# A row-sum kernel on one core: GpSimd scales the results, and the input is read in two parts at other pitches

## The chip, the core and the metric

The kernel runs on one core of a Trainium2 chip. VectorE, ScalarE and GpSimd are the engines that compute here. The DMA engines move data between HBM, where the input and the output lie, and SBUF, where the kernel's tiles of 128 partitions lie; SyncE issues these transfers. A load "lands" when all of its data has arrived. The metric is the device time of one execution in microseconds (us). The profile's span, from the first to the last instruction, is some 1.6 us shorter than that time (159.8 against 161.4 for the kernel before).

## The reference

```python
batch, seq, dim = 32, 512, 1024
x = np.random.randn(batch, seq, dim).astype(np.float32)
divisor = float(dim)
return (np.sum(x, axis=-1) / divisor).astype(np.float32)
```

There are 16,384 rows of 1024 float32, 64 MB (67.11 million bytes) in all. On 128 partitions that is 128 rows per partition. One row on every partition is 512 KB, and "one row" below means that.

## The kernel before

112 rows per partition come first, 448 KB apart from partition to partition. The last 16 rows per partition lie in a part of their own, 64 KB apart. All loads go through one queue (the page has one, q1, with 2592 packets, the stores among them). VectorE sums most rows, ScalarE some of the last, and a first store writes 112 columns while the last loads still arrive. The end is cut finely so that little work is left when the last byte lands.

```python
L = 16
M = J - L                                   # 112
x_main = bass.AP(tensor=x.tensor, offset=0, ap=[[M * D, P], [D, M], [1, D]])
x_last = bass.AP(tensor=x.tensor, offset=P * M * D, ap=[[L * D, P], [D, L], [1, D]])
main = [(2, 0)] + [(14, 0)] * 6 + [(14, 4), (12, 5)]      # (rows, of these on ScalarE)
last = [(8, 4), (4, 2), (2, 1)]
bulk = ctx.enter_context(tc.tile_pool(name="bulk", bufs=3))   # three large buffers
one = ctx.enter_context(tc.tile_pool(name="one", bufs=1))
res = one.tile([P, M], F32, name="res")
fin = one.tile([P, L], F32, name="fin")
q = one.tile([P, L], F32, name="q")
r = one.tile([P, L], F32, name="r")
nc.gpsimd.memset(r, 0.0)
# ... loads and sums; the 4-row and 2-row loads and the row below have tiles of pool "one"
c = 768
row = one.tile([P, D], F32, name="row")
load(row, x_last[:, j, :])
act_sum(r[:, j : j + 1], row[:, c:], by=scale)
nc.vector.reduce_sum(out=q[:, j : j + 1], in_=row[:, :c], axis=AX)
# ... the last row comes in three pieces: pa (448 columns), pb (256), pc (320)
nc.gpsimd.tensor_scalar_mul(out=res, in0=res, scalar1=scale)
tc.keep_in_program_order(nc.sync.dma_start(out=o_main, in_=res))
act_sum(pc[:, D - b : D - b + 1], pa)
nc.vector.reduce_sum(out=pc[:, D - b + 1 :], in_=pb, axis=AX)
nc.vector.scalar_tensor_tensor(out=fin[:, : L - 1], in0=q[:, : L - 1], scalar=scale,
                               in1=r[:, : L - 1], op0=MULT, op1=ADD)
nc.vector.tensor_scalar(out=scaled, in0=pc, scalar1=scale, scalar2=0.0, op0=MULT, op1=ADD,
                        accum_out=fin[:, L - 1 :])
tc.keep_in_program_order(nc.sync.dma_start(out=o_last, in_=fin))
```

Of the kernel before, what the change touches and what calls it, by code (L numbers as in the profile page):

```python
# [9 lines left out]
F32 = mybir.dt.float32  # L10
ADD = mybir.AluOpType.add
MULT = mybir.AluOpType.mult
# [55 lines left out]
def close_while_storing(nc, landed):  # L68


    body, end = nc.main_func.blocks[1], nc.main_func.blocks[-1]
    store = [i for i in body.instructions if i.engine == SP and type(i).__name__ == "InstDMACopy"][-1]
    (lane,) = store.sync_info.on_update
    drain = end.instructions[0]
    assert drain.engine == SP and type(drain).__name__ == "InstDrain"
    needs = {w.id: w for w in drain.sync_info.on_wait}
    assert needs[lane.id].wait_value > lane.update_value
    needs[lane.id] = dataclasses.replace(
        needs[lane.id], wait_value=needs[lane.id].wait_value - lane.update_value
    )  # L80

    (done,) = [w for w in store.sync_info.on_wait if w.ant_name.startswith("DVE_")]
    assert needs[done.id].wait_value == done.wait_value
    del needs[done.id]
    own = dict(sync_type="semaphore", id=landed.num, ant_name=landed.name)
    add = mybir.SyncUpdate(update_mode="sem-add-imm", update_value=16, **own)
    sub = mybir.SyncUpdate(update_mode="sem-sub-imm", update_value=16, **own)
    last = nc.sync.wait_ge(landed, 16).ins
    assert nc.main_func.blocks[-1].instructions[-1].name == last.name
    body.instructions = [i for i in body.instructions if i.name != store.name]  # L90
    end.instructions = [
        with_sync(drain, on_wait=tuple(needs.values())),
        with_sync(store, on_wait=(done,), on_update=(add,)),
        *end.instructions[1:-1],
        with_sync(last, on_update=(sub,)),
    ]


@with_exitstack
def kernel(  # L100
    ctx: ExitStack,
    tc: tile.TileContext,
    x: bass.AP,
    divisor: float,
    out: bass.AP,
):
    nc = tc.nc
    landed = nc.alloc_semaphore("landed")
    nc.at_finalize(start_loads_at_once)
    nc.at_finalize(latest_wait_first)  # L110
    nc.at_finalize(lambda nc: close_while_storing(nc, landed))
    xf = x.flatten_outer_dims()
    N, D = xf.shape
    P = nc.NUM_PARTITIONS
    scale = 1.0 / float(divisor)
    J = N // P
    assert J * P == N


    L = 16  # L120
    M = J - L
    x_main = bass.AP(tensor=x.tensor, offset=0, ap=[[M * D, P], [D, M], [1, D]])
    x_last = bass.AP(tensor=x.tensor, offset=P * M * D, ap=[[L * D, P], [D, L], [1, D]])
    o_main = bass.AP(tensor=out.tensor, offset=0, ap=[[M, P], [1, M]])
    o_last = bass.AP(tensor=out.tensor, offset=P * M, ap=[[L, P], [1, L]])


    main = [(2, 0)] + [(14, 0)] * 6 + [(14, 4), (12, 5)]
    last = [(8, 4), (4, 2), (2, 1)]
    assert sum(n for n, _ in main) == M and sum(n for n, _ in last) == L - 2  # L130
    bulk = ctx.enter_context(tc.tile_pool(name="bulk", bufs=3))
    one = ctx.enter_context(tc.tile_pool(name="one", bufs=1))
    psum = ctx.enter_context(tc.tile_pool(name="junk", bufs=4, space=bass.MemoryType.PSUM))

    res = one.tile([P, M], F32, name="res")
    fin = one.tile([P, L], F32, name="fin")
    q = one.tile([P, L], F32, name="q")
    r = one.tile([P, L], F32, name="r")
    nc.gpsimd.memset(r, 0.0)  # L139

    def load(dst, src):
        tc.keep_in_program_order(nc.sync.dma_start(out=dst, in_=src))  # L142

    def act_sum(dst, src, by=1.0):
        n = src.shape[-1]
        junk = psum.tile([P, D], F32, name="junk")
        nc.scalar.activation(junk[:, :n], src, COPY, scale=by, accum_out=dst)  # L147

    def sums(dst, t, rows, on_act):
        d = rows - on_act  # L150
        for i in range(d, rows):
            act_sum(dst[:, i : i + 1], t[:, i, :])
        nc.vector.reduce_sum(out=dst[:, :d], in_=t[:, :d, :], axis=AX)  # L153

    j = 0
    for rows, on_act in main:
        t = bulk.tile([P, 14, D], F32, name="t")
        load(t[:, :rows, :], x_main[:, j : j + rows, :])
        sums(res[:, j : j + rows], t, rows, on_act)
        j += rows  # L160
    j = 0
    for rows, on_act in last:
        if rows == 8:
            t = bulk.tile([P, 14, D], F32, name="t")[:, :8, :]
        else:
            t = one.tile([P, rows, D], F32, name=f"t{rows}")
        load(t, x_last[:, j : j + rows, :])
        sums(q[:, j : j + rows], t, rows, on_act)
        j += rows


    c = 768
    row = one.tile([P, D], F32, name="row")
    load(row, x_last[:, j, :])
    act_sum(r[:, j : j + 1], row[:, c:], by=scale)
    nc.vector.reduce_sum(out=q[:, j : j + 1], in_=row[:, :c], axis=AX)  # L176



    a, b = 448, 704  # L180
    pa = one.tile([P, a], F32, name="pa")
    pb = one.tile([P, b - a], F32, name="pb")
    pc = one.tile([P, D - b + 2], F32, name="pc")
    load(pa, x_last[:, L - 1, :a])
    load(pb, x_last[:, L - 1, a:b])
    load(pc[:, : D - b], x_last[:, L - 1, b:])


    nc.gpsimd.tensor_scalar_mul(out=res, in0=res, scalar1=scale)  # L189
    tc.keep_in_program_order(nc.sync.dma_start(out=o_main, in_=res))  # L190

    act_sum(pc[:, D - b : D - b + 1], pa)
    nc.vector.reduce_sum(out=pc[:, D - b + 1 :], in_=pb, axis=AX)  # L193
    nc.vector.scalar_tensor_tensor(  # L194
        out=fin[:, : L - 1], in0=q[:, : L - 1], scalar=scale, in1=r[:, : L - 1], op0=MULT, op1=ADD
    )
    scaled = one.tile([P, D - b + 2], F32, name="scaled")
    nc.vector.tensor_scalar(  # L198
        out=scaled, in0=pc, scalar1=scale, scalar2=0.0, op0=MULT, op1=ADD, accum_out=fin[:, L - 1 :]
    )  # L200
    tc.keep_in_program_order(nc.sync.dma_start(out=o_last, in_=fin))
# [35 lines left out]
```

## Time and profile before

| | before |
|---|---|
| time, median of the first 3 runs | 161.4 us |
| span of the profiled run | 159.8 us |
| read from HBM | 67.11 MB |
| VectorE / ScalarE / GpSimd busy | 76% / 12% / 0% |
| 14-row loads land every | 16.94 us |
| VectorE needs for one | 15.09 us |
| last full row lands at | 156.16 us |
| last VectorE result at | 158.28 us |

The busy shares name no bound. The landings do: where its engine is free, a load's first reader starts about 0.02 us after it lands, so the starts of the readers in the timeline are the clock of the transfer. The prediction shows these lines and reads them.

### The profile page before, as it was taken

Reading aid. Unit: us, or ns where it says so; the run is one execution under the profiler, and the core shown is the slowest. Engines: PE = TensorE matmul, PEld = TensorE weight load, DVE = VectorE, ACT = ScalarE, POOL = GpSimd, SP = SyncE. Lnnn points to the kernel's source line nnn. Section 1 sums busy time; section 2 is a strip of 40 time slices with the busy share of each in tenths; the row PEclk is TensorE's granted clock in tenths of the full one; section 3 lists DMA queues with packets and bytes.
Section 4 is the critical chain, followed back from the end, with each engine's and each line's share of the span. In section 5 each row is a group of like instructions: output and inputs, shape, how many; then the busy total and the mean of one; then the engine's idle time right before and its main releaser. Section 6 shows DMA issues by size and latency. Waiting matters only on the chain.

```text
span 159.8 us, 139 instructions
## 1 busy us (share of the span) xinstructions
DVE 121.1 (76%) x17; ACT 19.6 (12%) x37; POOL 0.8 (0%) x6
## 2 busy tenths in 40 slices
DVE  0500059995999599978999599959995996494985
ACT  3000000000000000000000000000001900480973
POOL 0000000000000000000000000000000000001000
DMA  7999999978999999978999999978999999899993
GB/s 250 472 459 459 459 459 459 459 330 359 459 459 459 459 459 459 459 316 373 459 459 459 459 459 459 416 345 388 459 459 427 394 480 505 353 435 390 408 400 132
DMA packets 2592, 67.18 MB, mean 420 GB/s; under 512 B 544, under 2 KB 928, under 8 KB 1056
## 3 DMA queue, kind: packets, MB, share of 16 engines
q1 hardware_dynamic: 2592, 67.18, 98.0%
HBM read 67.11 MB, written 0.07 MB: 420 GB/s over the span
## 4 chain that ended last, share of the span: by engine, by line
DMA 76%; DVE 22%; SPq 1%; issue 0%; DVEq 0%
DMA t<-in_x_dram 56%; DMA row<-in_x_dram 21%; DVE res L153 20%; SPq L142 1%; DVE q L176 1%; DVE scaled L198 0%; DVE pc L193 0%; DVE fin L194 0%; DVEq L198 0%; DVEq L232 0%
## 5 line engine op out<-in xcount | busy, mean ns | idle before, releaser
L153 DVE TENSOR_REDUCE res<-t 128x14 f32<-128x14336 f32 (+3 forms) x9 | 111.2, 12360 | 34.3 <-DMA t<-in_x_dram 34.3
L147 ACT ACTIVATE junk<-t 128x1024 f32<-128x1024 f32 x16 | 16.2, 1013 | 135.9 <-DMA t<-in_x_dram 135.9
L153 DVE TENSOR_REDUCE q<-t 128x4 f32<-128x4096 f32 (+2 forms) x3 | 7.9, 2642 | 2.7 <-DMA t<-in_x_dram 2.5
L147 ACT ACTIVATION_READ_ACCUMULATOR junk<-t 128x1 f32 x16 | 3.0, 187 | 0.0
L147 ACT ACT_TABLE_LOAD x1 | 1.3, 1283 | 1.7 <-PEq L218 1.7
L189 POOL TENSOR_SCALAR res<-res 128x112 f32<-128x112 f32 x1 | 0.5, 494 | 143.8 <-DVE res L153 143.8
L176 DVE TENSOR_REDUCE q<-row 128x1 f32<-128x768 f32 x1 | 1.0, 953 | 0.0
L198 DVE TENSOR_SCALAR_CACHE_REDUCE scaled<-pc 128x322 f32<-128x322 f32 x1 | 0.5, 490 | 0.1
L147 ACT ACTIVATE junk<-pa 128x448 f32<-128x448 f32 x1 | 0.5, 548 | 0.0
L193 DVE TENSOR_REDUCE pc<-pb 128x1 f32<-128x256 f32 x1 | 0.4, 414 | 0.0
L147 ACT ACTIVATE junk<-row 128x256 f32<-128x256 f32 x1 | 0.4, 388 | 0.1
L194 DVE SCALAR_TENSOR_TENSOR fin<-q,r 128x15 f32<-128x15 f32 x1 | 0.2, 176 | 0.0
L147 ACT ACTIVATION_READ_ACCUMULATOR junk<-pa 128x1 f32 x1 | 0.2, 186 | 0.0
L147 ACT ACTIVATION_READ_ACCUMULATOR junk<-row 128x1 f32 x1 | 0.2, 185 | 0.0
L139 POOL MEMSET r<- 128x16 f32 x1 | 0.1, 112 | 1.3 <-POOLq L218 1.3
L218 POOL MEMSET const-bfloat16-1.0<- 128x1 bf16 x1 | 0.1, 103 | 0.0
L218 POOL MEMSET const-uint8-127<- 128x1 uint8 x1 | 0.1, 102 | 0.0
L218 POOL MEMSET const-float32-0.0<- 128x1 f32 x1 | 0.1, 99 | 0.2 <-issue 0.2
L218 POOL MEMSET const-float32-1.0<- 128x1 f32 x1 | 0.1, 99 | 0.0
L198 DVE DVE_READ_ACCUMULATOR scaled<-pc 128x1 f32 x1 | 0.1, 83 | 0.0
## 6 DMA issues: line engine op xcount, KB each, us to landing
t<-in_x_dram SPq DMA_DIRECT2D x7, 7168.0 KB, 35.7
t<-in_x_dram SPq DMA_DIRECT2D x1, 6144.0 KB, 33.3
t<-in_x_dram SPq DMA_DIRECT2D x1, 4096.0 KB, 26.1
t<-in_x_dram SPq DMA_DIRECT2D x2, 1024.0 KB, 18.6
t<-in_x_dram SPq DMA_DIRECT2D x1, 2048.0 KB, 30.5
row<-in_x_dram SPq DMA_DIRECT2D x1, 512.0 KB, 33.2
pa<-in_x_dram SPq DMA_DIRECT2D x1, 224.0 KB, 33.3
pc<-in_x_dram SPq DMA_DIRECT2D x1, 160.0 KB, 33.1
```

The costliest lines, as they stand in the source:

```text
L139: nc.gpsimd.memset(r, 0.0)
L142: tc.keep_in_program_order(nc.sync.dma_start(out=dst, in_=src))
L147: nc.scalar.activation(junk[:, :n], src, COPY, scale=by, accum_out=dst)
L153: nc.vector.reduce_sum(out=dst[:, :d], in_=t[:, :d, :], axis=AX)
L176: nc.vector.reduce_sum(out=q[:, j : j + 1], in_=row[:, :c], axis=AX)
L189: nc.gpsimd.tensor_scalar_mul(out=res, in0=res, scalar1=scale)
L193: nc.vector.reduce_sum(out=pc[:, D - b + 1 :], in_=pb, axis=AX)
L194: nc.vector.scalar_tensor_tensor(out=fin[:, : L - 1], in0=q[:, : L - 1], scalar=scale, in1=r[:, : L - 1], op0=MULT, op1=ADD)
L198: nc.vector.tensor_scalar(out=scaled, in0=pc, scalar1=scale, scalar2=0.0, op0=MULT, op1=ADD, accum_out=fin[:, L - 1 :])
L218: nc = _bacc.Bacc("TRN2", target_bir_lowering=False, num_devices=1)
```

## The change

Its intent is to take two short things off the end of VectorE's work. GpSimd scales the last columns, and ScalarE takes 64 more columns of the last full row. It also rearranges which rows each partition reads. The first 16 rows per partition become a part of their own, 64 KB apart. The other 112 lie 448 KB apart, and their last 16 are the tail.

```diff
-    L = 16
-    M = J - L
-    x_main = bass.AP(tensor=x.tensor, offset=0, ap=[[M * D, P], [D, M], [1, D]])
-    x_last = bass.AP(tensor=x.tensor, offset=P * M * D, ap=[[L * D, P], [D, L], [1, D]])
+    F, L = 16, 16
+    M = J - F - L
+    W = M + L
+    x_first = bass.AP(tensor=x.tensor, offset=0, ap=[[F * D, P], [D, F], [1, D]])
+    x_main = bass.AP(tensor=x.tensor, offset=P * F * D, ap=[[W * D, P], [D, M], [1, D]])
+    x_last = bass.AP(tensor=x.tensor, offset=P * F * D + M * D, ap=[[W * D, P], [D, L], [1, D]])
 ... (outputs likewise; the loads are split into first and main, sizes and order kept)
+    res0 = one.tile([P, F], F32, name="res0")
     res = one.tile([P, M], F32, name="res")
-    r = one.tile([P, L], F32, name="r")
-    nc.gpsimd.memset(r, 0.0)
+    r = one.tile([P, 1], F32, name="r")
 ...
-    c = 768
+    c = 704
-    act_sum(r[:, j : j + 1], row[:, c:], by=scale)
+    act_sum(r, row[:, c:], by=scale)
 ...
+    tc.keep_in_program_order(nc.sync.dma_start(out=o_first, in_=res0))
     tc.keep_in_program_order(nc.sync.dma_start(out=o_main, in_=res))
 ...
-    nc.vector.scalar_tensor_tensor(
-        out=fin[:, : L - 1], in0=q[:, : L - 1], scalar=scale, in1=r[:, : L - 1], op0=MULT, op1=ADD
+    nc.gpsimd.tensor_scalar_mul(out=fin[:, :j], in0=q[:, :j], scalar1=scale)
+    nc.gpsimd.tensor_scalar(
+        out=fin[:, j : j + 1], in0=q[:, j : j + 1], scalar1=scale, scalar2=r, op0=MULT, op1=ADD
     )
```

More of the change, by code (lines that the diff above doesn't have):

```diff
@@ L117 @@
     assert J * P == N
-    L = 16
-    M = J - L
-    x_main = bass.AP(tensor=x.tensor, offset=0, ap=[[M * D, P], [D, M], [1, D]])
-    x_last = bass.AP(tensor=x.tensor, offset=P * M * D, ap=[[L * D, P], [D, L], [1, D]])
-    o_main = bass.AP(tensor=out.tensor, offset=0, ap=[[M, P], [1, M]])
-    o_last = bass.AP(tensor=out.tensor, offset=P * M, ap=[[L, P], [1, L]])
-    main = [(2, 0)] + [(14, 0)] * 6 + [(14, 4), (12, 5)]
+    F, L = 16, 16
[4 more added lines that the diff above has]
+    x_last = bass.AP(tensor=x.tensor, offset=P * F * D + M * D, ap=[[W * D, P], [D, L], [1, D]])
+    o_first = bass.AP(tensor=out.tensor, offset=0, ap=[[F, P], [1, F]])
+    o_main = bass.AP(tensor=out.tensor, offset=P * F, ap=[[W, P], [1, M]])
+    o_last = bass.AP(tensor=out.tensor, offset=P * F + M, ap=[[W, P], [1, L]])
+    first = [(2, 0), (14, 0)]
+    main = [(14, 0)] * 5 + [(14, 4), (12, 5)]
     last = [(8, 4), (4, 2), (2, 1)]
+    assert sum(n for n, _ in first) == F
     assert sum(n for n, _ in main) == M and sum(n for n, _ in last) == L - 2
@@ L153, in sums @@
         nc.vector.reduce_sum(out=dst[:, :d], in_=t[:, :d, :], axis=AX)
-    j = 0
-    for rows, on_act in main:
-        t = bulk.tile([P, 14, D], F32, name="t")
-        load(t[:, :rows, :], x_main[:, j : j + rows, :])
-        sums(res[:, j : j + rows], t, rows, on_act)
-        j += rows
+    for loads, src, dst in ((first, x_first, res0), (main, x_main, res)):
+        j = 0
+        for rows, on_act in loads:
+            t = bulk.tile([P, 14, D], F32, name="t")
+            load(t[:, :rows, :], src[:, j : j + rows, :])
+            sums(dst[:, j : j + rows], t, rows, on_act)
+            j += rows
+        nc.gpsimd.tensor_scalar_mul(out=dst, in0=dst, scalar1=scale)
     j = 0
@@ L186 @@
     load(pc[:, : D - b], x_last[:, L - 1, b:])
-    nc.gpsimd.tensor_scalar_mul(out=res, in0=res, scalar1=scale)
+    tc.keep_in_program_order(nc.sync.dma_start(out=o_first, in_=res0))
     tc.keep_in_program_order(nc.sync.dma_start(out=o_main, in_=res))
```

## The prediction

> **What bounds the kernel now.** I read the page first (busy shares and bytes), then the timeline for the moments at which loads land, then the chain of work that ended last for the tail, then the SyncE queue's own waits for the end of the program. The page:
>
> ```profile
> span 159.8 us, 139 instructions
> ...
> DVE 121.1 (76%) x17; ACT 19.6 (12%) x37; POOL 0.8 (0%) x6
> ...
> HBM read 67.11 MB, written 0.07 MB: 420 GB/s over the span
> ```
>
> No engine is full: VectorE has a quarter of the span free, GpSimd is idle. What is large is the bytes. Whether the transfers stream without a hole is read from the timeline, because each reduction starts as its load lands:
>
> ```profile
> 4.83 2.29 DVE L153 TENSOR_REDUCE res<-t 128x2 f32<-128x2048 f32 x1 [4.83 <-DMA t<-in_x_dram]
> 21.76 15.09 DVE L153 TENSOR_REDUCE res<-t 128x14 f32<-128x14336 f32 x1 [14.65 <-DMA t<-in_x_dram]
> 38.71 15.09 DVE L153 TENSOR_REDUCE res<-t 128x14 f32<-128x14336 f32 x1 [1.87 <-DMA t<-in_x_dram]
> ...
> 106.47 15.09 DVE L153 TENSOR_REDUCE res<-t 128x14 f32<-128x14336 f32 x1 [1.85 <-DMA t<-in_x_dram]
> ...
> 137.94 7.62 DVE L153 TENSOR_REDUCE res<-t 128x7 f32<-128x7168 f32 x1 [3.72 <-DMA t<-in_x_dram]
> ...
> 147.66 4.42 DVE L153 TENSOR_REDUCE q<-t 128x4 f32<-128x4096 f32 x1 [2.09 <-DMA t<-in_x_dram]
> ```
>
> From 21.76 to 106.47 five loads of 14 rows land, 16.94 us each. That is 1.210 us a row (512 KB over all partitions), 7,340,032 bytes / 16.94 us = 433 GB/s. VectorE needs 15.09 for what takes 16.94 to arrive, and waits some 1.85 us for each load. The tail keeps the same pace: the 8-row load lands 147.66 - 137.94 = 9.72 us after the one before it, 1.215 a row; and that one already comes from the part whose partitions lie 64 KB apart. So the kernel is one unbroken transfer: 128 rows x 1.210 = 154.9 us, before it 4.83 - 2 x 1.210 = 2.41 us until the stream is at its pace, and after it a tail. 2.41 + 154.9 = 157.3; the rest of 159.8, 2.5 us, is what the kernel does after its last byte.
>
> The head, in the view by windows (columns: window, length, busy time of DVE, ACT and POOL, clock, DMA share, GB/s):
>
> ```profile
> 0.00:2.00 2.00, 0.00 (x0) 0.26 (x1) 0.30 (x5) 1.00 0.49 90
> 2.00:4.00 2.00, 0.00 (x0) 1.02 (x1) 0.00 (x0) 1.00 0.97 410
> ```
>
> In the first two microseconds the DMA engines are half busy and move little. The trace's records of single packets say why: the first 8 KB packet of each engine takes 0.43 to 1.29 us, from the third on each takes 0.31. The slowest engine loses about 1 us there[...]. The tail, in the chain (start, us, what):
>
> ```profile
> 122.91 33.25 DMA row<-in_x_dram
> ...
> 156.18 0.96 DVE q L176
> 157.14 0.03 issue
> 157.17 0.18 DVE fin L194
> 157.34 0.34 DVE pc L193
> 157.68 0.04 DVEq L198
> 157.72 0.07 issue
> 157.79 0.49 DVE scaled L198
> ```
>
> VectorE carries four instructions in a row after the landing of the last full row at 156.16. The final store is issued at 158.31 and lands about 1.4 us later. Before it, the SyncE queue also waits for the earlier transfers:
>
> ```profile
> SPq L190 <- DMA t<-in_x_dram: 13.1, 1, 13.1
> ...
> SPq L232 <- DMA out_dram<-res: 0.6, 1, 0.6
> ...
> SPq L201 <- DVE scaled L198: 0.5, 1, 0.5
> ```
>
> The last line is the slack: all other transfers were done 0.5 us before the last VectorE result.
>
> [...]
>
> **The change, part by part.**
> *Bulk.* The loads keep their sizes and order (2, seven of 14, 12, 8, 4, 2, 1, and the last row in three pieces), the tiles and the three buffers too. Only addresses change. The first 16 rows get the 64 KB pitch that the last 16 had, the last 16 the 448 KB pitch that the main part had. Both pitches run at full rate in the trace. Effect: 0 us.
>
> *Head.* The first packets now touch 128 places in 8 MB instead of 56 MB. If the slow first packets depend on how far apart the places are, up to a few tenths change; if they are a cold start of the engines, nothing. I take -0.05 us.
>
> *Scaling of the first part.* One small GpSimd instruction near 37 us instead of its share of the one at 145.65. Off the path: 0 us. The store of the first part is one more transfer. The 13.1 us wait above shows a store that waits for a load eight transfers before it (the one that landed at 137.94). So the new first store will wait until about 137.9 and the main store until the 8-row load at 147.7, instead of 146.17. [...]the main store landed at about 157.7. Eight more packets of 64 bytes per engine at 11 ns each (packet records) put it at 157.8. The final store is not ready before 158.1, so this is hidden: 0 us.
>
> *Tail on VectorE.* Removed: the 176 ns multiply-add, of which about 0.09 us stands on the path, since the next reduction starts 0.09 after it (157.26 against 157.17). Shortened: the row reduction from 768 to 704 columns. With 1220 ns at 1024 and 953 at 768 a column costs 1.04 ns, so 64 columns give 0.07 us: 953 becomes 886. ScalarE takes 320 instead of 256 columns; with 388 ns at 256 and 548 at 448 that is 441 ns. It ends near 156.62, and its next instruction moves from 156.72 to about 156.77, its result from 157.39 to about 157.44. New times: row reduction 156.18 to 157.07; reduction of pb (landed near 157.0) 157.10 to 157.51; scaled, 0.12 after it as before, from 157.63 (pc landed near 157.5) to 158.12. Before: 158.28. Gain: 0.16 us.
>
> *Tail on GpSimd.* The 14 scaled columns can start when the one-row reduction is done, near 156.2. The last column's multiply-add starts after the row reduction, near 157.15. From 494 ns for 112 columns, and 112 ns for a memset of 16 columns, I estimate 0.25 to 0.45 us for each. The last ends at 157.4 to 157.6, half a microsecond before 158.12: hidden.
>
> *Final store.* 64 bytes per partition as before, but 448 bytes apart instead of side by side. I expect its landing within 0.1 us of 1.4.
>
> Sum: -0.05 - 0.16 = -0.21 us. Span 159.55; time 161.4 - 0.2 = 161.2 us.
>
> **The rivals.**
> *GpSimd sets the end.* If its last instruction took over 0.9 us, or if the framework made VectorE's write of the last column wait for GpSimd's writes to the same tile, the end would move to about 158.5 or later: +0.2 to +0.6, 161.6 to 162.0. Against it: at 123.41 ScalarE and VectorE write columns of the same tile together, so columns are kept apart, and 494 ns for eight times the columns leaves room.
> *The 64 KB pitch hurts the large pieces.* The last part read 32 KB pieces and smaller at that pitch; now 56 KB pieces are read.[...] Against it: 9.72 us for eight rows at that pitch.
> *A better head or tail.* The 4 KB packets of the last full row took 172 ns on average where the quickest took 159: 13 ns x 8 = 0.1 us per engine, at the 64 KB pitch. A wider pitch may take that away, and a tighter one may spare half of the lost 1 us at the head: 160.6 to 161.0.
>
> **Range and chances.** [...]the result can leave 161.4 only by the head (at most 1 us) and the tail (some tenths). Runs of before lie within 0.17 us. I predict 161.2, range 160.6 to 161.7. Faster by 2% means below 158.2; the data alone end at 157.3 in the span, and the time is 1.6 us more than the span (161.4 against 159.8), which makes 158.9 even without a tail: 0.01. Slower by 2% means over 164.6, which only the pitch rival gives: 0.01. Same: 0.98.
>
> **What would show it.** In the changed profile: 14-row loads 16.94 us apart, also the first; first load near 4.8; row reduction near 886 ns; the reduction of pb right behind it; scaled ending near 158.1; the final store released by VectorE, not GpSimd or a store; span near 159.6. Wrong if a landing interval exceeds 1.22 us a row (pitch), if the first landing moves by over 0.3 us (head), or if GpSimd stands in the chain at the end.

The forecast's sum came to -0.21 us, -0.05 from the head (a guess) and -0.16 from the tail on VectorE. That no layout could make the bulk faster was the assumption. The trace shows 1.210 us a row (433 GB/s) at 448 KB and 1.215 at 64 KB, and these are the "full rate" under *Bulk*. No measured figure stands behind the 64 KB rival's time over 164.6.

## The result, and the profile after

The changed kernel took 161.37 us (median of 6 runs, 161.22 to 161.61) and the kernel before 161.31 (6 runs, 161.25 to 161.51). The ratio is 1.0002, with a 95% interval of 0.999 to 1.0015: the same. A ratio here is the mean time of one kernel's fast runs over that of the other's of the same rounds, so it is not quite the ratio of the medians. Executions over 1.5% slower than the fastest of the same kernel are left out of the means.

The changed kernel's page:

```profile
span 159.9 us, 143 instructions
...
DVE 121.0 (76%) x16; ACT 19.7 (12%) x37; POOL 1.4 (1%) x8
...
HBM read 67.11 MB, written 0.07 MB: 420 GB/s over the span
```

VectorE has one instruction less and GpSimd two more. The bytes are the same. The timeline of the changed kernel (start, us, engine, line, operation, output from input, count, idle time before and what ended it), at the head and at the end:

```profile
4.92 2.29 DVE L158 TENSOR_REDUCE res<-t 128x2 f32<-128x2048 f32 x1 [4.92 <-DMA t<-in_x_dram]
21.86 15.09 DVE L158 TENSOR_REDUCE res<-t 128x14 f32<-128x14336 f32 x1 [14.66 <-DMA t<-in_x_dram]
38.81 15.09 DVE L158 TENSOR_REDUCE res<-t 128x14 f32<-128x14336 f32 x1 [1.86 <-DMA t<-in_x_dram]
...
147.76 4.42 DVE L158 TENSOR_REDUCE q<-t 128x4 f32<-128x4096 f32 x1 [2.09 <-DMA t<-in_x_dram]
...
152.65 2.29 DVE L158 TENSOR_REDUCE q<-t 128x2 f32<-128x2048 f32 x1 [0.47 <-DMA t<-in_x_dram]
...
155.15 1.22 DVE L158 TENSOR_REDUCE q<-t 128x1 f32<-128x1024 f32 x1 [0.21 <-DMA t<-in_x_dram]
...
156.46 0.89 DVE L183 TENSOR_REDUCE q<-row 128x1 f32<-128x704 f32 x1
```

The bulk is as before: 14-row loads 16.94 to 16.95 us apart, also in the part at 64 KB. The tail is not. From the 8-row load on, the next three landings come 4.89, 2.50 and 1.31 us apart. Before they were 4.84, 2.42 and 1.26. There the readers of these loads started at 147.66 and 156.18 (both in the prediction's lines), and between them on ScalarE:

```profile
152.49 1.03 ACT L147 ACTIVATE junk<-t 128x1024 f32<-128x1024 f32 x1 [0.57 <-DMA t<-in_x_dram]
...
154.92 1.03 ACT L147 ACTIVATE junk<-t 128x1024 f32<-128x1024 f32 x1 [0.24 <-DMA t<-in_x_dram]
```

The chain of the changed kernel shows what the later landings do to the end (start, us, what):

```profile
123.98 33.43 DMA pb<-in_x_dram
...
157.43 0.43 DVE pc L200
...
157.97 0.49 DVE scaled L206
```

The reduction of pb now waits for a landing (157.41) where it should have followed VectorE's own work. The row reduction is shorter and ended at 156.46 + 0.89 = 157.35, but pb was not there yet.

The book of the two profiled runs, up to the end of `scaled` (158.28 before, 158.46 after, so +0.18):

- First landing: 4.83 to 4.92, +0.09.
- From the first landing to the start of the row reduction: 151.35 to 151.54, +0.19.
- From there to the end of `scaled`: 2.10 to 2.00, -0.10.

So the end did become shorter, and the transfers took the gain back before it. The question for the experiments is what made them later.

### The profile page after: what moved, and what is told of

It is laid out like the page before. It is cut to its first block, busy times and chain, and to the rows that moved or that the text cites. A ratio compares the mean times of both kernels' runs of the same rounds, so it can differ in the third digit from the quotient of the medians.

```text
span 159.9 us, 143 instructions
## 1 busy us (share of the span) xinstructions
DVE 121.0 (76%) x16; ACT 19.7 (12%) x37; POOL 1.4 (1%) x8
## 4 chain that ended last, share of the span: by engine, by line
DMA 77%; DVE 21%; SPq 1%; issue 0%; DVEq 0%
DMA t<-in_x_dram 56%; DMA pb<-in_x_dram 21%; DVE res L158 20%; SPq L147 1%; DVE scaled L206 0%; DVE pc L200 0%; DVEq L206 0%; DVEq L240 0%
## 5 line engine op out<-in xcount | busy, mean ns | idle before, releaser
L167 POOL TENSOR_SCALAR res<-res 128x16 f32<-128x16 f32 (+1 forms) x2 | 0.7, 354 | 145.1 <-DVE res L158 145.1
L183 DVE TENSOR_REDUCE q<-row 128x1 f32<-128x704 f32 x1 | 0.9, 885 | 0.1
```

The lines of the kernel that those rows point to most:

```text
L167: nc.gpsimd.tensor_scalar_mul(out=dst, in0=dst, scalar1=scale)
```

## The experiments

Three theories were on the table first. A: the new addresses make the small pieces of the tail slower. B: the landings set the end anyway, and the work taken off VectorE was never worth anything. C: the later landings were chance. "Landings" below are the three intervals after the 8-row load (of the 4-row, the 2-row and the one-row load), read from the starts of their readers.

### The end alone, and the addresses alone

`tail_only` is the kernel before with the change's end and nothing of its layout:

```diff
-    r = one.tile([P, L], F32, name="r")
-    nc.gpsimd.memset(r, 0.0)
+    r = one.tile([P, 1], F32, name="r")
-    c = 768
+    c = 704
-    nc.vector.scalar_tensor_tensor(out=fin[:, : L - 1], ...)
+    nc.gpsimd.tensor_scalar_mul(out=fin[:, :j], in0=q[:, :j], scalar1=scale)
+    nc.gpsimd.tensor_scalar(out=fin[:, j : j + 1], ..., scalar2=r, op0=MULT, op1=ADD)
```

> Addresses, parts and stores of before; only the end is that of the change (GpSimd scales the last 15 columns, row split at 704). Theory A, the gain on VectorE is real and the new addresses took it back: row reduction about 885 ns, reduction of pb right behind it near 157.1, scaled ends near 158.1, time 0.16 us under before (ratio about 0.999). Rival B, the landing of the last pieces sets the end and the VectorE work was never worth anything: the reduction of pb starts later than the row reduction lets it, and the ratio is 1.000 within 0.0005.

Measured: 161.44 us against 161.41, ratio 1.0001 (0.9988 to 1.0013).

`layout_only` is the changed kernel with the end of before:

```diff
-    r = one.tile([P, 1], F32, name="r")
+    r = one.tile([P, L], F32, name="r")
+    nc.gpsimd.memset(r, 0.0)
-    c = 704
+    c = 768
-    nc.gpsimd.tensor_scalar_mul(...); nc.gpsimd.tensor_scalar(...)
+    nc.vector.scalar_tensor_tensor(out=fin[:, : L - 1], ...)
```

> New parts, addresses and stores; the end is that of before (multiply-add on VectorE, row split at 768). Theory A: the last row lands near 156.4 instead of 156.16 and pb near 157.4 instead of 157.0, so scaled ends near 158.5 to 158.6 and the time is 0.2 us over before (ratio about 1.0015). Rival C, the later landings of the first profile were chance of that one execution: landings as before and ratio 1.000.

Measured: 161.22 us against 161.41, ratio 0.999 (0.9976 to 1.0004). The timelines turn theory A upside down. First the end alone, on the old addresses:

```profile
147.66 4.42 DVE L152 TENSOR_REDUCE q<-t 128x4 f32<-128x4096 f32 x1 [2.09 <-DMA t<-in_x_dram]
...
152.57 2.29 DVE L152 TENSOR_REDUCE q<-t 128x2 f32<-128x2048 f32 x1 [0.49 <-DMA t<-in_x_dram]
...
155.06 1.22 DVE L152 TENSOR_REDUCE q<-t 128x1 f32<-128x1024 f32 x1 [0.20 <-DMA t<-in_x_dram]
...
156.35 0.89 DVE L175 TENSOR_REDUCE q<-row 128x1 f32<-128x704 f32 x1
```

Then the new addresses with the old end (ScalarE's lines, since VectorE was still busy when the 2-row load landed):

```profile
152.46 1.03 ACT L153 ACTIVATE junk<-t 128x1024 f32<-128x1024 f32 x1 [0.56 <-DMA t<-in_x_dram]
...
154.88 1.03 ACT L153 ACTIVATE junk<-t 128x1024 f32<-128x1024 f32 x1 [0.23 <-DMA t<-in_x_dram]
...
156.11 0.39 ACT L153 ACTIVATE junk<-row 128x256 f32<-128x256 f32 x1
```

The late landings (4.91, 2.49, 1.29) are there without the new addresses. They are gone (4.83, 2.42, 1.23, with the 8-row load at 147.63) with the new addresses and the old end. So theory A falls, and so does C. Something in the code of the end slows transfers that land before any instruction of that end has run.

### Two more layouts

`three_parts` gives the tail back a part of its own at 64 KB, with the middle 96 rows 384 KB apart. `pitch512` makes it one part of 128 rows, 512 KB apart. Both keep the change's end.

```diff
-    x_main = ... offset=P * F * D, ap=[[W * D, P], ...
-    x_last = ... offset=P * F * D + M * D, ap=[[W * D, P], ...
+    x_main = ... offset=P * F * D, ap=[[M * D, P], ...            # three_parts
+    x_last = ... offset=P * (F + M) * D, ap=[[L * D, P], ...
+    x_first, x_main, x_last = ... offset=0 / F * D / (F + M) * D, ap=[[J * D, P], ...   # pitch512
```

> The change with its last 16 rows back in a part of their own at 64 KB; first 16 rows at 64 KB as in the change, middle 96 rows at 384 KB. Tells head from tail. If the small pieces at the wide pitch are what lands late (theory A), the 4-, 2- and 1-row loads land 4.84, 2.43 and 1.26 us apart as before (not 4.89, 2.50, 1.31 as in the change) and the time is 0.15 to 0.2 us under the change, about 161.2. If the late landing comes with the first part or with one store more, it stays at about 161.4.

Measured: 161.71 us against 161.41, ratio 1.0015 (1.0002 to 1.0028); landings 4.89, 2.50, 1.30. The tail's pitch went back to 64 KB and the landings stayed late, a second time against theory A. In its profile the 12-row load also came 14.68 us after the one before it (14.53 before). Why is open, and with it why this kernel is a little slower than the changed one.

> What the split into parts avoids: one part of 128 rows per partition, 512 KB apart, same loads and the end of the change.[...] If reads from HBM have slack enough at this pitch, they stay 16.94 apart and the time is about 161.3.

Measured: 161.55 us against 161.41, ratio 1.0012 (0.9997 to 1.0027). The pitch that the split into parts avoids costs the bulk nothing; the timeline of this run:

```profile
21.75 15.09 DVE L158 TENSOR_REDUCE res<-t 128x14 f32<-128x14336 f32 x1 [14.62 <-DMA t<-in_x_dram]
38.69 15.09 DVE L158 TENSOR_REDUCE res<-t 128x14 f32<-128x14336 f32 x1 [1.85 <-DMA t<-in_x_dram]
```

Again 16.94 us per load, and again late landings in the tail (4.90, 2.50, 1.28).

### What the four slow tails share: where their tiles lie

All four kernels with the change's end have `r` as one column, and the others have 16. The tiles of pool "one" follow each other in a partition's SBUF. The tiles' addresses in the built programs (they are not in the traces) show that `r` starts at byte 189,120 in both kernels. With 64 bytes for `r`, the tile of the 4-row load starts at 189,184, which is 739 x 256. With 4 bytes (rounded up to 32) it starts at 189,152, 224 past a multiple of 256. The 2-row tile, row, pa, pb and pc follow it with sizes that are multiples of 256, so all six move together.

That made theory D: the start of the destination tiles costs the time. Which boundary would count, 64 bytes or 256, two of the runs below tell. The rival E was that the GpSimd instructions or the shorter reduction do. The first test adds columns to `r` and nothing else:

```diff
-    r = one.tile([P, 1], F32, name="r")
+    r = one.tile([P, 16], F32, name="r")[:, :1]      # after_r16: tail at 0 past a multiple of 256
+    r = one.tile([P, 48], F32, name="r")[:, :1]      # after_r48: tail at 128 past
```

> The change with r held in a tile of 16 columns, of which one is used, so that the tail's tiles again start at a multiple of 64 bytes (of 256) in a partition's SBUF. Theory D, the late landings come from tiles that start 32 bytes past a multiple of 64: the 4-, 2- and 1-row loads land 4.83, 2.42 and 1.25 us apart, the reduction of pb follows the row reduction at once, scaled ends near 158.05, time about 161.05, ratio about 0.998. Rival E, the GpSimd instructions or the shorter row reduction themselves delay the transfers: landings 4.89, 2.50, 1.30 apart as in the change, ratio about 1.000.

Measured: 161.05 us against 161.35, ratio 0.9974 (0.9961 to 0.9988). The timeline:

```profile
152.50 2.29 DVE L158 TENSOR_REDUCE q<-t 128x2 f32<-128x2048 f32 x1 [0.42 <-DMA t<-in_x_dram]
...
154.94 1.22 DVE L158 TENSOR_REDUCE q<-t 128x1 f32<-128x1024 f32 x1 [0.15 <-DMA t<-in_x_dram]
...
156.16 0.89 DVE L183 TENSOR_REDUCE q<-row 128x1 f32<-128x704 f32 x1
...
157.03 0.42 DVE L200 TENSOR_REDUCE pc<-pb 128x1 f32<-128x256 f32 x1
...
157.57 0.49 DVE L206 TENSOR_SCALAR_CACHE_REDUCE scaled<-pc 128x322 f32<-128x322 f32 x1
```

The 8-row load landed at 147.66, so the landings are 4.84, 2.44 and 1.22 again. The reduction of pb follows the row reduction at once, and `scaled` ends at 158.06. GpSimd's last instruction ends at 157.41, 0.65 us earlier.

> As the run before it, with r in a tile of 48 columns: the tail's tiles start at a multiple of 64 bytes, but 128 past a multiple of 256. If only the 64-byte boundary counts, landings and time as with 16 columns (4.83, 2.42, 1.25; about 161.05). If the 256-byte boundary counts,[...] landings nearer 4.89, 2.50, 1.30 and about 161.3.

Measured: 161.31 us against 161.35, ratio 0.9992 (0.998 to 1.0005); landings 4.89, 2.49, 1.29. So a multiple of 64 bytes is not enough, nor one of 128; with tiles on a multiple of 256 `after_r16` had 4.84, 2.44 and 1.22. The counter-test moves the tiles of the kernel before and changes nothing else in it:

```diff
     nc.gpsimd.memset(r, 0.0)
+    spare = one.tile([P, 8], F32, name="spare")
+    nc.gpsimd.memset(spare, 0.0)
```

> The kernel before with nothing changed but an unused tile of 8 columns between r and the tail's tiles, which moves them 32 bytes on. Theory D: the 4-, 2- and 1-row loads land 4.89, 2.50, 1.30 apart instead of 4.84, 2.43, 1.26, scaled ends 0.2 to 0.25 later, time 161.55 to 161.65, ratio about 1.0015. Rival E: no change, ratio 1.000.

Measured: 161.57 us against 161.35, ratio 1.0008 (0.9995 to 1.002). The median is 0.2 up, but the interval of the ratio does not exclude 1. The profile is clear: landings 4.89, 2.51, 1.30, and `scaled` ends at 158.54 instead of 158.28.

```profile
147.75 4.42 DVE L155 TENSOR_REDUCE q<-t 128x4 f32<-128x4096 f32 x1 [2.11 <-DMA t<-in_x_dram]
...
152.64 1.03 ACT L149 ACTIVATE junk<-t 128x1024 f32<-128x1024 f32 x1 [0.63 <-DMA t<-in_x_dram]
...
155.15 1.22 DVE L155 TENSOR_REDUCE q<-t 128x1 f32<-128x1024 f32 x1 [0.22 <-DMA t<-in_x_dram]
...
156.45 0.95 DVE L178 TENSOR_REDUCE q<-row 128x1 f32<-128x768 f32 x1
```

With no GpSimd instruction at the end and the row split at 768, rival E is out. The trace's records of single packets show the price in five of the six late kernels: a 16 KB packet took 612.5 to 614 ns in the median instead of 611, a packet of pc 59.5 to 60 instead of 55. `three_parts` is the exception: 611 and 55 with tiles 224 past the boundary, and landings as late. So longer packets are not the whole of the mechanism, which stays open.

### What the price grows with

The price in the tail is about 0.06 us for each of the loads of 2 MB, 1 MB and 512 KB (mean of the late kernels less that of the others). Among these three it goes with the load, not with its bytes. Each load is 128 pieces, one per partition (128 packets each of 16, 8 and 4 KB for these three in the trace of the kernel before). The page counts 16 DMA engines, and a 56 KB piece in 2.116 us is 27.1 GB/s, a sixteenth of the stream's 433: some eight pieces of a load to each engine (an estimate). The three large buffers start 128 past a multiple of 256 in every kernel so far, so one run moves them to 160 past, and two move them to a multiple:

```diff
+    front = ctx.enter_context(tc.tile_pool(name="front", bufs=1))
+    spare = front.tile([P, 8], F32, name="spare")    # bulk_off32; [P, 32] in the two all256
+    nc.gpsimd.memset(spare, 0.0)
     bulk = ctx.enter_context(tc.tile_pool(name="bulk", bufs=3))
 ...
 ... (r widened to 72 or 48 columns, so that the tail's tiles stay on a multiple of 256)
```

> The kernel before with its three large buffers moved 32 bytes past a multiple of 64 and the tail's tiles on a multiple of 256. It tells what the price of the 32 bytes grows with. If it is per load (about 0.06 us each, as in the tail), ten loads through these buffers cost 0.5 to 0.6 us: 14-row loads 17.0 apart, time about 161.9. If it grows with the bytes (0.06 to 0.07 us on the 2 MB and 1 MB loads, that is 1.2 to 2.9 per cent), 14-row loads land 17.1 to 17.4 apart and the time is 163 to 165.

Measured: 161.36 us against 161.35, ratio 0.9999 (0.9986 to 1.0011), 14-row loads 16.94 apart. Nothing was added, but the large buffers had been off the boundary already, so this run could not tell per load from per byte. Its expectation missed that.

> The change with r in 48 columns and an unused tile of 32 columns ahead of the three large buffers: all load destinations start at a multiple of 256 bytes; until now the large buffers lay 128 bytes past one in every kernel but one (160 there, same time). If a start off that boundary costs 0.05 to 0.07 us per load wherever it lies, the ten loads through the large buffers save 0.5 to 0.7 us on top of the 0.3 of the run with 16 columns: 14-row loads 16.87 apart, time 160.4 to 160.6, ratio about 0.994 to 0.995. If the price holds only for the small tiles, 16.94 apart and 161.05.

Measured: 160.95 us against 161.34, ratio 0.9973 (0.9958 to 0.9988).

> The kernel before with only its three large buffers moved to a multiple of 256 bytes (the tail's tiles are there already). Price per load: 14-row loads 16.87 apart, time 160.7 to 160.9, ratio about 0.996. Price only for small tiles: 161.35, ratio 1.000.

Measured: 161.17 us against 161.34, ratio 0.9988 (0.9973 to 1.0002). The large loads gained less than half of what was expected, as the timeline of `after_all256` has it:

```profile
21.60 15.09 DVE L161 TENSOR_REDUCE res<-t 128x14 f32<-128x14336 f32 x1 [14.62 <-DMA t<-in_x_dram]
38.51 15.09 DVE L161 TENSOR_REDUCE res<-t 128x14 f32<-128x14336 f32 x1 [1.83 <-DMA t<-in_x_dram]
```

That is 16.91 apart, not 16.87, and some of it is lost again in the tail (4.89, 2.47, 1.24, with tiles on a multiple of 256). From the first landing to the row reduction this kernel took 151.23 us, against 151.31 with 16 columns: 0.08 gained where 0.5 to 0.7 were expected. A 56 KB piece took 2.116 us in the median in either place.

The large loads did pay something. From the first landing to that of the 8-row load, `after_all256` took 142.63 us (142.82 with 16 columns) and `before_all256` 142.60 (142.83 before). That is 0.19 and 0.23 us over ten loads, so some 0.02 us each. The price per load is smaller on large pieces.

The tail of these two kernels (8.60 and 8.64 us from the 8-row load to the row reduction) lies between the two groups, but its transfers are not slower. In `after_all256` and `after_r16` alike, the packets of 16, 8 and 4 KB took 611, 309 and 159 ns in the median, and the last packet of the row ended 8.56 us after the last one of the 8-row load. What differs is the time from a load's last packet to its landing. For the 8-row load it was 0.30 us in `after_all256` and 0.45 in `after_r16`, for the row 0.34 and 0.38. The 8-row load had landed early, so the tail had less to win back. Whether moving the large buffers is worth anything beyond the noise is open.

### How much is the end, and how much the layout

`tail_r16` is `tail_only` with `r` in 16 columns, as above.

> Addresses, parts and stores of before, the end of the change, r in a tile of 16 columns: the tail's tiles start at a multiple of 256 bytes. If the reworked end alone is worth the 0.16 us worked out in the prediction, scaled ends near 158.1, time about 161.15, ratio 0.998 to 0.999, and what the change with 16 columns has beyond that (161.05) is worth of the layout, at most 0.1 us. If the layout of addresses matters, this run stays at about 161.3.

Measured: 161.10 us against 161.34, ratio 0.9985 (0.9968 to 1.0002); `scaled` ends at 158.06 instead of 158.28. So theory B falls too: with the data in time, the work taken off VectorE is worth something. With the tail's tiles on a multiple of 256 the four combinations are:

| ratio to before | end of before | end of the change |
|---|---|---|
| addresses of before | 1 | 0.9985 (161.10 us) |
| addresses of the change | 0.999 (161.22 us) | 0.9974 (161.05 us) |

The new end is worth about 0.2 us by the medians and in the profiles; the interval of `tail_r16` alone reaches 1.0002. The layout may be worth up to 0.2 or nothing: its interval alone reaches 1.0004. In the profiles the first load lands at 4.67 to 4.92 us in the six kernels whose first part is at 64 KB (mean 4.79), and at 4.83 to 5.00 in the six at 448 KB (mean 4.88). The ranges overlap.

## Why the prediction was right or wrong

The time is right: 161.37 lies in 160.6 to 161.7, 0.2 above the point, and the call "same" holds. That range holds a change worth nothing as well as the forecast gain, so the time alone does not confirm the working of the tail. The reason that is left for the missing 2%, that the stream of bytes at 433 GB/s is the kernel, holds too: the mean interval of the 14-row loads stayed between 16.91 and 16.95 us in all 13 kernels (434 to 433 GB/s). That these runs stand at a limit of the hardware was not shown. The small gain that was forecast did not appear, and one step of the working is why.

- **Bulk: right for the reads, wrong in one clause.** The step said that the loads keep "the tiles and the three buffers too. Only addresses change", with the effect put at 0 us. The HBM addresses did cost the bulk nothing, even at 512 KB (16.94 us per 14-row load in `pitch512`). But the destinations of the tail moved as well: shrinking `r` from 16 columns to one shifted six tiles off a multiple of 256 bytes. The profiles put the price at 0.19 us between the first landing and the row reduction. With `r` at 16 columns again it is gone. One sign of being wrong that the prediction set, over 1.22 us a row between landings, did appear (2.50 for two rows, 1.31 for one). But it was meant for the pitch, and the kernel before already had 1.26 for one row.
- **Tail on VectorE: right, and shown.** 0.16 us was worked out. Where the data came in time, the stretch from the row reduction to the end of `scaled` went from 2.10 to 1.90 us (`after_r16` and `tail_r16`), 0.20. The row reduction took 885 ns (886 forecast). In the changed kernel itself only 0.10 came through, mostly because pb landed 0.06 us after VectorE was free. The shift of ScalarE's next instruction to 156.77 did not come: in `after_r16` it started at 156.72 as before, since pa landed only at 156.69.
- **Tail on GpSimd: right.** The two instructions took 262 and 267 ns (0.25 to 0.45 estimated). GpSimd's last one ended at 157.72, against 158.46 for `scaled`. The operations of before, 494 ns for 112 columns on GpSimd and 176 for 15 on VectorE, do not separate a fixed part from the columns. The new ones do: 260 ns for 16 columns and 449 for 96 leave some 0.22 us for none (an estimate).
- **Head: not resolved.** -0.05 was forecast. The profiled run had +0.09, six against six profiles give -0.09, and single profiles spread by 0.25 or less.
- **Stores: right, but the late tail moved them.** The lines of SyncE's waits in the changed kernel (who waited for what, us in total, times, longest) show it:

```profile
SPq L197 <- DMA t<-in_x_dram: 9.3, 1, 9.3
...
SPq L240 <- DMA out_dram<-res: 1.1, 1, 1.1
```

The main store was held until the 8-row load had landed, as forecast, and it landed at 158.21, not 157.8. The last load itself landed at 157.81 instead of 157.50, and the store 0.40 us behind it instead of 0.21. Where the tail was not late (`after_r16`), the store landed at 157.78, 0.33 behind the last load (0.22 with one store, `tail_r16`): the forecast's 0.1 us for a second store. With one store SyncE had 0.3 us left before `scaled`, with two 0.2. It stayed hidden, and the final store landed 1.4 us after its issue, as forecast.
- **The rivals.** GpSimd at the end and the 64 KB pitch did not come about, as argued (the 14-row load at 64 KB landed 16.94 us after the one before it). The third, that a wider pitch takes away the slow 4 KB packets of the last row, is not shown. In the changed kernel they took 162 ns on average instead of 172, but at the old 64 KB pitch they took 159 in `bulk_off32` and 161.5 in `tail_r16`, so the 172 does not belong to the pitch. The other packets of the tail took longer in the changed kernel, by 0.5 to 6 ns. The forecast had a list of what the diff removes, and the resized `r` was in the diff. It was read as arithmetic and not as placement.

## What to carry to other kernels

In a kernel that is one stream of bytes, look at where the destination tiles start as well as at the source addresses: a helper tile that is made smaller can move every tile after it, and loads into them may then cost more (here 0.19 us of 161 in the tail). Here the stretch from the 8-row load to the row reduction took 8.48 to 8.52 us with the tail's tiles on a multiple of 256 bytes and 8.67 to 8.70 off one (8.60 and 8.64 with the large buffers on a multiple too), so try that placement, most of all for the small loads at the end, and check it after every edit of the tiles around them. When a change that shortens the end gives nothing, compare the landings before looking at the engines: the work here did get shorter, and its data came later by the same amount.

## What these runs measured

- With tail tiles 32, 128 or 224 bytes past a multiple of 256, from the 8-row load to the row reduction took 8.67 to 8.70 us in six kernels. With them on a multiple (and the large buffers off one), it took 8.48 to 8.52 in five. What in the transfers makes the difference was not shown.
- The price was smaller for large pieces. Loads of 4 to 16 KB pieces paid about 0.06 us each; loads of 56 KB pieces gained 0.02 to 0.03 us of 16.94 when their buffers were moved onto a multiple of 256 bytes.
- Loads from HBM to SBUF ran at 433 GB/s with partitions 512 KB apart (16.94 us for 7,340,032 bytes), as at 448 KB.
- On GpSimd, multiplications of 14, 16 and 96 columns took 262, 260 and 449 ns, a multiply-add of one column with a per-partition addend 267.
